# Prologue of a hybrid encoder layer: loads, statistics, normalisation, transposes and splits in another order

## The chip, the cores and the metric

The kernel runs on one core of one Trainium2 chip. The metric is the device time of one execution in microseconds (us). Three executions before the change took 1594.86, 1594.96 and 1596.01 us, with a median of 1594.96 us.

## The reference

The input x has 256 tokens of 4096 numbers in float32. It is normalised over its 4096 numbers per token (the embedding LayerNorm), goes through one layer, and is normalised again. Cut to what matters:

```python
h = layer_norm(x, emb_ln_g, emb_ln_b)
p = h @ w_in                       # (256, 4096) @ (4096, 13312)
# 16 channel groups of a gated short convolution, 16 attention heads (4 kv heads, window 128)
y_conv = c_b * centred_short_conv(c_c * c_h, conv_w) * silu(c_z)
y_attn = banded_window_attention(a_q, a_k, a_v, sink) * silu(a_z)
y = concatenate([y_conv, y_attn]) @ w_out     # (256, 4096) @ (4096, 4096)
out = layer_norm(2 ** 0.25 * h + y, ln_g, ln_b)
```

## The kernel before

The 256 tokens are two token tiles of 128 partitions, `xs[0]` and `xs[1]`, each of 128x4096. The transposed, normalised stream lies in `hT` as 32 blocks of 128 channels by 256 tokens. Matmuls contract over these blocks, and each result of 128 tokens by 512 columns is summed up in one PSUM accumulator over all 32 blocks.

The weights come in pieces of 1 MB (`load`, line 68): 128 partitions by 2048 numbers, that is, four blocks of 128 channels by 512 columns. Eight pieces make one chunk of 512 columns. A piece is split (`split`, line 77) into a high part `whi`, written by ScalarE (line 83), and a low part `wlo`, which VectorE makes by subtraction (line 85). The stream is split in the same way into `xT` (`x_split`, lines 206 and 207, both on VectorE). `mm` (line 105) then takes three matmuls for each block and token tile, in float32r (lines 116 to 118): 24 matmuls for one piece. For the raw pieces, the high parts and the low parts there are three buffers each.

The first two pieces are not split. They are loaded into two of the buffers of `whi` (the tiles `first`), and `first_mm` (line 198) multiplies them in plain float32 (line 201) with `hT`: `first_mm(q, i)` is piece q with token tile i, four matmuls, each of which the profile records twice. So pieces 0 and 1 need `hT` alone, and piece 2 is the first that needs `xT`, `whi` and `wlo`.

The order of the work is written out by hand: the program runs on each engine in the order of the code, and tiles carry the semaphores. The change touches the prologue, lines 135 to 262:

- `x_load(i)`, line 141: five loads of a token tile, all by SP's queue, in pieces of 1024, 1024, 1024, 512 and 512 columns. The weights come through the same queue. SP issues a load only when the eighth load before it has landed.
- `stats(i, c)`, line 161: VectorE's statistics of 512 columns, eight for a token tile. `stats_end(i)`, line 164: the aggregate, and `small_chain` (line 121), a chain of tiny instructions with one square root on ScalarE (line 124).
- `norm(i, q)`, line 168: 512 columns of a token tile are normalised in place, on VectorE or on GpSimd (line 170).
- `transp(i, q)`, line 173: TensorE turns four blocks of one token tile (line 177), and ScalarE takes each out of PSUM with the LayerNorm's gain and bias (line 180). `transp2(q)`, line 184: the same for both token tiles at once, with eight transposes (line 189) and four ScalarE instructions of twice the width (line 192).
- Two matmuls at line 214 run ahead of the transposes, for no result that is used.

In the order before, token tile 0 is normalised by VectorE (q = 0 to 2) and GpSimd (q = 3 to 7). VectorE takes the statistics of tile 1 in between, and their square root stands on ScalarE behind all sixteen instructions that take tile 0's first four groups out of PSUM. After the transposes of groups 0 to 3 of both tiles and the four `first_mm`, VectorE splits group 2 of the stream and piece 2 of the weights, and only then normalises the second half of tile 1 (the second `for q` over `norm(1, q)`). From piece 2 on, every step is `transp2` of a later group, `mm`, `x_split`, `split` and `load`.

Of the kernel before, what the change touches and what calls it, by code (L numbers as in the profile page):

```python
# [44 lines left out]
def encoder_kernel(ctx: ExitStack, tc: tile.TileContext, x, emb_g, emb_b, wi, conv_w, sink, wo, ln_g, ln_b, out):  # L45
    nc = tc.nc
# [5 lines left out]
    ps_acc = ctx.enter_context(tc.tile_pool(name="ps_acc", bufs=4, space=PSUM))  # L52
# [16 lines left out]
    def load(j, to=None):  # L69
        if j >= len(steps):  # L70
            return
        kind, a, b = steps[j]
        if to is None:
            to = raw[j] = wpool.tile([P, PIECE], F32, name="wraw")
        nc.sync.dma_start(out=to, in_=wi[a, b] if kind == "in" else wo[a + b])

    def split(j):
        if j >= len(steps):
            return
        w = raw.pop(j)  # L80
        over = j == len(steps) - 1
        wh[j] = wpool.tile([P, PIECE], F32R, name="whi", tag="wraw" if over else "whi")
        nc.scalar.activation(wh[j], w, AF.Copy)  # L83
        wl[j] = wpool.tile([P, PIECE], F32R, name="wlo", tag="wraw" if over else "wlo")
        nc.vector.tensor_tensor(wl[j], w, wh[j].bitcast(F32), op=ALU.subtract)  # L85


    ident = const.tile([P, P], F32, name="ident")
# [14 lines left out]
    acc = {}  # L103
# [31 lines left out]
    with tc.tile_pool(name="pro", bufs=1) as pro:  # L135
# [11 lines left out]
        nc.sync.dma_start(out=g_c, in_=emb_g)  # L147
        nc.sync.dma_start(out=b_c, in_=emb_b)
        load(0, first[0])
        x_load(1)  # L150
        load(1, first[1])
        for j in range(2, 4):
            load(j)
        nc.sync.dma_start(out=cw, in_=conv_w)
# [10 lines left out]
            nc.vector.bn_aggr(musd[:, i, 0:2], st[i])  # L165
            small_chain(musd[:, i:i + 1, :], 1)

        def norm(i, q, eng=None):
            sl = slice(q * 512, (q + 1) * 512)
            (eng or nc.vector).tensor_scalar(xs[i][:, sl], xs[i][:, sl], musd[:, i, 0:1], musd[:, i, 2:3],  # L170
                                             op0=ALU.subtract, op1=ALU.mult)

        def transp(i, q):
            pt = ps_att.tile([P, 4, P], F32, name="att")
            for k in range(4):
                kt = q * 4 + k
                nc.tensor.transpose(pt[:, k, :], xs[i][:, kt * P:(kt + 1) * P], ident)  # L177
            for k in range(4):
                kt = q * 4 + k
                nc.scalar.activation(hT[:, kt, i * P:(i + 1) * P], pt[:, k, :], AF.Identity, scale=g_c[:, kt:kt + 1],  # L180
                                     bias=b_c[:, kt:kt + 1])

        def transp2(q):
            for half in range(2):
                pt = ps_att.tile([P, 2, S], F32, name="att")
                for k in range(2):
                    kt = q * 4 + half * 2 + k
                    for i in range(2):
                        nc.tensor.transpose(pt[:, k, i * P:(i + 1) * P], xs[i][:, kt * P:(kt + 1) * P], ident)  # L189
                for k in range(2):  # L190
                    kt = q * 4 + half * 2 + k
                    nc.scalar.activation(hT[:, kt, :], pt[:, k, :], AF.Identity, scale=g_c[:, kt:kt + 1],
                                         bias=b_c[:, kt:kt + 1])
# [4 lines left out]
        def first_mm(q, i):  # L198
            for k in range(PK):
                kt = q * PK + k  # L200
                nc.tensor.matmul(acc[0, i], hT[:, kt, i * P:(i + 1) * P], first[q][:, k * W:(k + 1) * W],  # L201
                                 start=(kt == 0), stop=False)
# [9 lines left out]
        wu = ps_att.tile([P, 512], F32, name="att")  # L212
        for _ in range(2):
            nc.tensor.matmul(wu, ident, xs[0][:, 3072:3584], start=True, stop=True)
        for q in range(3, NQ):
            norm(0, q, nc.gpsimd)
        norm(0, 0)
        transp(0, 0)
        norm(0, 1)
        transp(0, 1)  # L220
        for c in range(NQ):
            stats(1, c)
            if c in (0, 2):
                if c == 0:
                    norm(0, 2)
                first_mm(c // 2, 0)
                transp(0, c // 2 + 2)
        stats_end(1)
        for q in range(NQ // 2):
            norm(1, q)  # L230
        transp(1, 0)
        transp(1, 1)
        first_mm(0, 1)
        transp(1, 2)
        transp(1, 3)
        first_mm(1, 1)
        x_split(2)
        split(2)
        load(5)
        for q in range(NQ // 2, NQ):  # L240
            norm(1, q)
        transp2(4)
        x_split(3)
        split(3)
        load(6)
        mm(2)
        transp2(5)
        x_split(4)
        split(4)
        load(7)  # L250
        mm(3)
        transp2(6)
        x_split(5)
        split(5)
        load(8)
        mm(4)
        transp2(7)
        x_split(6)
        split(6)
        load(9)  # L260
        mm(5)
        x_split(7)
        split(7)
        load(10)
# [407 lines left out]
```

## Time and profile before

| | |
|---|---|
| median of three executions | 1594.96 us |
| the profiled execution's own time | 1595.1 us |
| its span, from the first to the last instruction | 1593.4 us |
| matmuls on TensorE (PE) | 98% of the span |
| weight loads on TensorE (PEld) | 81% |
| VectorE (DVE) | 52% |
| ScalarE (ACT) | 39% |
| GpSimd (POOL) | 1% |
| read from HBM | 299.99 MB |

The profile comes from one execution. Its span lies 1.7 us under that execution's own time. "L118" is line 118 of the kernel. PE's rows are matmuls, PEld's are the loads of the stationary operand, SPq is the queue of SyncE, which issues the loads. A row of the timeline gives the start, the duration, the engine, the line, and what is written from what; at the end stands the idle time before it with what ended it. "PEclk" is the clock granted to TensorE as a share of full speed.

### The profile page before, as it was taken

The numbers are of one execution on the slowest core, as the hardware profiler recorded it, in microseconds if no ns is written. First come the engines' busy times: TensorE is split into PE (matmuls) and PEld (weight loads), VectorE is DVE, ScalarE is ACT, GpSimd is POOL, SyncE is SP. The second block draws the span as 40 slices with busy tenths as digits, with TensorE's granted clock in tenths as the row PEclk, the third lists the DMA queues.
The fourth block names the chain that finished last, engine by engine and source line by source line (L and its number), as shares of the span: only waits on it lengthen the run. The fifth ranks groups of instructions, "written<-read, shape, count | busy, mean of one in ns | idle before, by whom it ended". The sixth has DMA issues, their size and how long they took to land.

```text
span 1593.4 us, 16893 instructions
## 1 busy us (share of the span) xinstructions
PE 1567.2 (98%) x7182; PEld 1290.1 (81%) x7182; DVE 833.4 (52%) x702; ACT 620.3 (39%) x511; POOL 12.0 (1%) x12
## 2 busy tenths in 40 slices
PE   6999999999999999999999999999999999999997
PEld 3788888888888888888888888888888888888896
DVE  4754455464554645444544445444546556656656
ACT  3533435353444433333333333333344333333331
POOL 2000000000000000000000000000000000000000
PEclk9999999999999999999999999999999999999998
DMA  6555545545455455555555555555555657666662
GB/s 239 182 192 196 189 144 186 199 152 184 149 188 185 165 184 192 196 185 185 172 209 199 186 185 185 193 189 198 180 191 185 225 196 261 218 226 226 228 218 106
DMA packets 49515, 305.36 MB, mean 192 GB/s; under 512 B 6080, under 2 KB 7584, under 8 KB 14624
## 3 DMA queue, kind: packets, MB, share of 16 engines
q1 hardware_dynamic: 48864, 302.72, 54.6%
q10 hardware_dynamic: 576, 1.57, 0.3%
q8 instruction: 56, 0.92, 0.2%
q14 instruction: 19, 0.16, 0.0%
HBM read 299.99 MB, written 4.19 MB: 191 GB/s over the span
## 4 chain that ended last, share of the span: by engine, by line
PE 97%; DMA 1%; DVE 1%; ACT 0%; SPq 0%; issue 0%; DVEq 0%
PE acc L116 24%; PE acc L118 24%; PE acc L117 23%; PE acc L541 7%; PE acc L543 7%; PE acc L542 7%; PE att L305 1%; DMA first<-in_wi 1%; PE acc L201 1%; PE att L379 0%; DMA x<-in_x 0%; DVE R L576 0%; ACT hT L180 0%; PE att L189 0%; PE att L351 0%; PE att L390 0%
## 5 line engine op out<-in xcount | busy, mean ns | idle before, releaser
L85 DVE TENSOR_TENSOR wlo<-wraw,whi 128x2048 fp32r<-128x2048 f32 x270 | 618.0, 2291 | 628.7 <-ACT whi L83 628.6
L83 ACT ACTIVATE whi<-wraw 128x2048 fp32r<-128x2048 f32 x270 | 516.0, 1913 | 701.7 <-PE acc L118 439.9
L116 PE MATMUL acc<-whi,xT 128*128 128x512 f32 x1648 | 650.5, 395 | 0.0
L118 PE MATMUL acc<-whi,xT 128*128 128x512 f32 x1648 | 646.9, 393 | 0.0
L117 PE MATMUL acc<-wlo,xT 128*128 128x512 f32 x1648 | 641.8, 389 | 0.0
L118 PEld LDWEIGHTS acc<-whi,xT 128*128 128x128 f32 x1648 | 309.6, 188 | 70.6
L117 PEld LDWEIGHTS acc<-wlo,xT 128*128 128x128 f32 x1648 | 309.8, 188 | 68.1 <-DVE wlo L85 0.4
L116 PEld LDWEIGHTS acc<-whi,xT 128*128 128x128 f32 x1648 | 310.1, 188 | 61.9
L541 PE MATMUL acc<-whi,xT 128*128 128x512 f32 (+1 forms) x576 | 212.6, 369 | 0.0
L543 PE MATMUL acc<-whi,xT 128*128 128x512 f32 (+1 forms) x576 | 211.3, 367 | 0.0
L542 PE MATMUL acc<-wlo,xT 128*128 128x512 f32 (+1 forms) x576 | 209.8, 364 | 0.0
L543 PEld LDWEIGHTS acc<-whi,xT 128*128 128x128 f32 x576 | 108.0, 188 | 19.6
L542 PEld LDWEIGHTS acc<-wlo,xT 128*128 128x128 f32 x576 | 108.1, 188 | 19.1 <-DVE wlo L85 0.3
L541 PEld LDWEIGHTS acc<-whi,xT 128*128 128x128 f32 x576 | 108.3, 188 | 17.4 <-issue 0.7
L365 ACT ACTIVATE p<-s,nm 128x256 f32<-128x256 f32 x32 | 16.0, 502 | 59.8 <-DVE nm L360 59.8
L413 ACT ACTIVATE t<-att,cw 128x256 f32<-128x256 f32 x16 | 7.2, 474 | 26.8 <-PE att L305 16.1
L201 PE MATMUL acc<-first,hT 128*128 128x512 f32 x32 | 15.9, 640 | 1.2 <-DMA first<-in_wi 1.2
L180 ACT ACTIVATE hT<-att,b_c,g_c 128x128 f32<-128x128 f32 x32 | 11.7, 466 | 13.5 <-PE att L177 13.5
L391 DVE TENSOR_TENSOR Ya<-att,zT 128x256 f32<-128x256 f32 x16 | 6.7, 420 | 15.0 <-PE att L390 15.0
L414 DVE SCALAR_TENSOR_TENSOR t<-att,cw,t 128x255 f32<-128x255 f32 x16 | 7.7, 480 | 13.2 <-ACT t L413 13.2
L356 DVE SCALAR_TENSOR_TENSOR s<-tab,att 128x512 f32<-128x512 f32 x16 | 10.9, 681 | 5.8 <-PE att L353 5.8
L367 DVE TENSOR_TENSOR den<-den,es 128x2 f32<-128x2 f32 x16 | 2.6, 161 | 21.6 <-ACT es L366 21.6
(120 smaller groups left out, 473.7 us busy)
## 6 DMA issues: line engine op xcount, KB each, us to landing
wraw<-in_wi SPq DMA_DIRECT2D x206, 1024.0 KB, 4.9
wraw<-in_wo SPq DMA_DIRECT2D x64, 1024.0 KB, 5.0
xc<-in_x SPq DMA_DIRECT2D x14, 256.0 KB, 6.2
x<-in_x SPq DMA_DIRECT2D x6, 512.0 KB, 7.1
first<-in_wi SPq DMA_DIRECT2D x2, 1024.0 KB, 8.8
out<-R SPq DMA_DIRECT2D x4, 512.0 KB, 2.7
gb<-in_emb_g_row SPq DMA_DIRECT2D x7, 256.0 KB, 3.2
gb<-in_emb_b_row SPq DMA_DIRECT2D x7, 256.0 KB, 4.1
```

What stands on the lines that cost most here:

```text
L83: nc.scalar.activation(wh[j], w, AF.Copy)
L85: nc.vector.tensor_tensor(wl[j], w, wh[j].bitcast(F32), op=ALU.subtract)
L116: nc.tensor.matmul(a, xh, hk, start=(kt == 0), stop=False)
L117: nc.tensor.matmul(a, xh, lk, start=False, stop=False)
L118: nc.tensor.matmul(a, xl, hk, start=False, stop=(kt == KT - 1))
L180: nc.scalar.activation(hT[:, kt, i * P:(i + 1) * P], pt[:, k, :], AF.Identity, scale=g_c[:, kt:kt + 1], bias=b_c[:, kt:kt + 1])
L201: nc.tensor.matmul(acc[0, i], hT[:, kt, i * P:(i + 1) * P], first[q][:, k * W:(k + 1) * W], start=(kt == 0), stop=False)
L305: nc.tensor.transpose(ps[:, c, i * P:(i + 1) * P], t[:, i, (2 * b + c) * P:(2 * b + c + 1) * P], ident)
L365: nc.scalar.activation(p[:, b, :], s[:, b, :], AF.Exp, bias=nm[:, b:b + 1], accum_out=den[:, b:b + 1])
L541: nc.tensor.matmul(o, yh, hk, start=(s == 0), stop=False)
L542: nc.tensor.matmul(o, yh, lk, start=False, stop=False)
L543: nc.tensor.matmul(o, yl, hk, start=False, stop=(s == KT - 1))
```

## The change

Five things move; no arithmetic changes.

1. `split` becomes two functions, `split_hi` (ScalarE) and `split_lo` (VectorE), which can stand apart.
2. The load of the second `first` piece stands ahead of the five loads of token tile 1.
3. `norm` always runs on VectorE. All of tile 0 is normalised ahead of the statistics of tile 1, and all of tile 1 directly behind them.
4. `transp` only transposes, and `turned1` takes its PSUM tile out. For tile 1 those PSUM tiles come from the accumulators' pool. `transp2` can do one token tile at a time; `turned2` takes the pair out. Groups 2 and 3 are now turned by `transp2`, tile 0's half ahead of tile 1's statistics' end, tile 1's half later; before, `transp` did them.
5. From group 4 on, `transp2(q)` on TensorE keeps its place ahead of `mm(q - 2)`, but `turned2(q)` now stands behind that `mm` in the code, just ahead of `x_split(q)`. On ScalarE, `split_hi(2)` stands ahead of what takes tile 1 out of PSUM.

```diff
         load(0, first[0])
+        load(1, first[1])
         x_load(1)
-        load(1, first[1])
...
+        def turned1(i, q, pt):
             for k in range(4):
                 kt = q * 4 + k
                 nc.scalar.activation(hT[:, kt, i * P:(i + 1) * P], pt[:, k, :], AF.Identity, scale=g_c[:, kt:kt + 1],
                                      bias=b_c[:, kt:kt + 1])
...
+        def transp2(q, tiles=(0, 1)):
             for half in range(2):
-                pt = ps_att.tile([P, 2, S], F32, name="att")
+                if tiles[0] == 0:
+                    pair[q, half] = ps_att.tile([P, 2, S], F32, name="att")
...
-        for q in range(3, NQ):
-            norm(0, q, nc.gpsimd)
-        norm(0, 0)
-        transp(0, 0)
-        norm(0, 1)
-        transp(0, 1)
+        t0 = []
+        for q in range(2):
+            norm(0, q)
+            t0.append(transp(0, q, ps_att, "att"))
+        for q in range(2):
+            turned1(0, q, t0[q])
+            first_mm(q, 0)
+        for q in range(2, NQ):
+            norm(0, q)
         for c in range(NQ):
             stats(1, c)
-            if c in (0, 2):
-                if c == 0:
-                    norm(0, 2)
-                first_mm(c // 2, 0)
-                transp(0, c // 2 + 2)
+        transp2(2, (0,))
+        transp2(3, (0,))
         stats_end(1)
-        for q in range(NQ // 2):
+        split_hi(2)
+        for q in range(NQ):
             norm(1, q)
-        transp(1, 0)
-        transp(1, 1)
+        t1 = [transp(1, q, ps_acc, "acc") for q in range(2)]
+        transp2(2, (1,))
+        turned1(1, 0, t1[0])
         first_mm(0, 1)
-        transp(1, 2)
-        transp(1, 3)
+        transp2(3, (1,))
+        turned1(1, 1, t1[1])
         first_mm(1, 1)
+        turned2(2)
+        split_lo(2)
+        load(5)
         x_split(2)
-        split(2)
-        load(5)
-        for q in range(NQ // 2, NQ):
-            norm(1, q)
-        transp2(4)
+        turned2(3)
         x_split(3)
         split(3)
         load(6)
+        transp2(4)
         mm(2)
-        transp2(5)
+        turned2(4)
         x_split(4)
```

In the rows below, `x_88` and `x_89` are the token tiles 0 and 1, `first_91` and `first_92` the first two pieces of weights, `att` the PSUM tiles of transposes and `acc` the accumulators. The changed kernel's line numbers are shifted. TensorE before, from the first transposes to the transposes of group 4 (the row of L189 stands for the first of eight):

```order
L177 MATMUL att<-ident,x_88 128x128 x8
L201 MATMUL acc<-first_91,hT 128x512 x4
L177 MATMUL att<-ident,x_88 128x128 x4
L201 MATMUL acc<-first_92,hT 128x512 x4
L177 MATMUL att<-ident,x_88 128x128 x4
L177 MATMUL att<-ident,x_89 128x128 x8
L201 MATMUL acc<-first_91,hT 128x512 x4
L177 MATMUL att<-ident,x_89 128x128 x8
L201 MATMUL acc<-first_92,hT 128x512 x4
L189 MATMUL att<-ident,x_88 128x128
```

TensorE now, in the same place (L182 and L200 are the transposes, L217 is `first_mm`):

```order
L182 MATMUL att<-ident,x_88 128x128 x8
L217 MATMUL acc<-first_91,hT 128x512 x4
L217 MATMUL acc<-first_92,hT 128x512 x4
L200 MATMUL att<-ident,x_88 128x128 x8
L182 MATMUL acc<-ident,x_89 128x128 x8
L200 MATMUL att<-ident,x_89 128x128 x4
L217 MATMUL acc<-first_91,hT 128x512 x4
L200 MATMUL att<-ident,x_89 128x128 x4
L217 MATMUL acc<-first_92,hT 128x512 x4
L200 MATMUL att<-ident,x_88 128x128
```

Both pieces of tile 0 are multiplied in one go, and tile 0's groups 2 and 3 are turned behind them. ScalarE before, from the first square root to the first high part of weights:

```order
L124 ACTIVATE sd<-musd,eps_t 128x1
L180 ACTIVATE hT<-att,b_c,g_c 128x128 x16
L124 ACTIVATE sd<-musd,eps_t 128x1
L180 ACTIVATE hT<-att,b_c,g_c 128x128 x16
L83 ACTIVATE whi<-wraw 128x2048
L192 ACTIVATE hT<-att,b_c,g_c 128x256 x4
```

ScalarE now, in the same place (L129 is the square root, L80 the high part):

```order
L129 ACTIVATE sd<-musd,eps_t 128x1
L188 ACTIVATE hT<-att,b_c,g_c 128x128 x8
L129 ACTIVATE sd<-musd,eps_t 128x1
L80 ACTIVATE whi<-wraw 128x2048
L188 ACTIVATE hT<-acc,b_c,g_c 128x128 x8
L208 ACTIVATE hT<-att,b_c,g_c 128x256 x8
L80 ACTIVATE whi<-wraw 128x2048
```

The square root of tile 1 now has eight instructions ahead of it instead of sixteen, and the first high part stands ahead of tile 1's eight. VectorE before, from tile 0's normalisation to the second half of tile 1's, without the small chain:

```order
L170 TENSOR_SCALAR x_88<-x_88,musd 128x512 x2
L162 BN_STATS st_116<-x_89 128x6
L170 TENSOR_SCALAR x_88<-x_88,musd 128x512
L162 BN_STATS st_116<-x_89 128x6 x7
...
L170 TENSOR_SCALAR x_89<-x_89,musd 128x512 x4
L206 CAST xT<-hT 128x4x256
L207 TENSOR_TENSOR xT<-hT,xT 128x4x256
L85 TENSOR_TENSOR wlo<-wraw,whi 128x2048
L170 TENSOR_SCALAR x_89<-x_89,musd 128x512 x4
```

VectorE now, in the same place:

```order
L175 TENSOR_SCALAR x_88<-x_88,musd 128x512 x8
L167 BN_STATS st_116<-x_89 128x6 x8
...
L175 TENSOR_SCALAR x_89<-x_89,musd 128x512 x8
L85 TENSOR_TENSOR wlo<-wraw,whi 128x2048
L222 CAST xT<-hT 128x4x256
L223 TENSOR_TENSOR xT<-hT,xT 128x4x256
L222 CAST xT<-hT 128x4x256
L223 TENSOR_TENSOR xT<-hT,xT 128x4x256
L85 TENSOR_TENSOR wlo<-wraw,whi 128x2048
```

The eight normalisations of tile 1 stand together, ahead of the first low part and the first split of the stream.

More of the change, by code (lines that the diff above doesn't have):

```diff
@@ L75, in load, with split_hi, split_lo, split @@
         nc.sync.dma_start(out=to, in_=wi[a, b] if kind == "in" else wo[a + b])
[L77 to L80, printed above, removed]
+    def split_hi(j):
         over = j == len(steps) - 1
         wh[j] = wpool.tile([P, PIECE], F32R, name="whi", tag="wraw" if over else "whi")
-        nc.scalar.activation(wh[j], w, AF.Copy)
+        nc.scalar.activation(wh[j], raw[j], AF.Copy)
+    def split_lo(j):
+        over = j == len(steps) - 1
         wl[j] = wpool.tile([P, PIECE], F32R, name="wlo", tag="wraw" if over else "wlo")
-        nc.vector.tensor_tensor(wl[j], w, wh[j].bitcast(F32), op=ALU.subtract)
+        nc.vector.tensor_tensor(wl[j], raw.pop(j), wh[j].bitcast(F32), op=ALU.subtract)
+    def split(j):
+        if j < len(steps):
+            split_hi(j)
+            split_lo(j)
     ident = const.tile([P, P], F32, name="ident")
@@ L166, in stats_end, with norm, transp @@
             small_chain(musd[:, i:i + 1, :], 1)
-        def norm(i, q, eng=None):
+        def norm(i, q):
             sl = slice(q * 512, (q + 1) * 512)
[L170 to L174, printed above, removed]
+            nc.vector.tensor_scalar(xs[i][:, sl], xs[i][:, sl], musd[:, i, 0:1], musd[:, i, 2:3],
+                                    op0=ALU.subtract, op1=ALU.mult)
+        def transp(i, q, pool, name):
+            pt = pool.tile([P, 4, P], F32, name=name)
             for k in range(4):
@@ L177, in transp @@
                 nc.tensor.transpose(pt[:, k, :], xs[i][:, kt * P:(kt + 1) * P], ident)
+            return pt
+        def turned1(i, q, pt):
             for k in range(4):
@@ L181, in transp, with turned2 @@
                                      bias=b_c[:, kt:kt + 1])
-        def transp2(q):
+        pair = {}
+        def transp2(q, tiles=(0, 1)):
             for half in range(2):
-                pt = ps_att.tile([P, 2, S], F32, name="att")
+                if tiles[0] == 0:
+                    pair[q, half] = ps_att.tile([P, 2, S], F32, name="att")
                 for k in range(2):
                     kt = q * 4 + half * 2 + k
-                    for i in range(2):
-                        nc.tensor.transpose(pt[:, k, i * P:(i + 1) * P], xs[i][:, kt * P:(kt + 1) * P], ident)
+                    for i in tiles:
+                        nc.tensor.transpose(pair[q, half][:, k, i * P:(i + 1) * P], xs[i][:, kt * P:(kt + 1) * P],
+                                            ident)
+        def turned2(q):
+            for half in range(2):
+                pt = pair.pop((q, half))
                 for k in range(2):
@@ L250, in encoder_kernel @@
         load(7)
+        transp2(5)
         mm(3)
-        transp2(6)
+        turned2(5)
         x_split(5)
@@ L255, in encoder_kernel @@
         load(8)
+        transp2(6)
         mm(4)
-        transp2(7)
+        turned2(6)
         x_split(6)
@@ L260, in encoder_kernel @@
         load(9)
+        transp2(7)
         mm(5)
+        turned2(7)
         x_split(7)
```

## The prediction

> **What bounds the kernel now.** I read the page first, then the waits by engine, then the stretch in which TensorE waits: its timeline, the chain of work that ended last, and the timelines of VectorE and ScalarE.
>
> ```profile
> span 1593.4 us, 16893 instructions
> ...
> PE att L214 <- DMA x<-in_x: 8.9, 1, 8.9
> PE att L189 <- DVE x L170: 3.6, 1, 3.6
> PE att L177 <- DVE x L170: 3.2, 1, 3.2
> PE att L568 <- DVE t L563: 3.2, 1, 3.2
> PE acc L201 <- DMA first<-in_wi: 1.2, 1, 1.2
> ...
> 100.00:200.00 100.00, 100.00 (x443) 82.15 (x442) 42.88 (x21) 38.91 (x25) 0.00 (x0) 1.00 0.55 190
> ```
>
> The five middle rows are TensorE's waits over the whole run: microseconds in total, times, longest. The last row is a stage in the middle: 100 of 100 us busy at a granted clock of 1.00, VectorE and ScalarE under half. So outside the prologue and the tail nothing but TensorE's own work counts. The wait at L568 is in the tail, the 8.9 us at L214 are the first load; the change touches neither. It can win only the other three waits, 3.6 + 3.2 + 1.2 = 8.0 us, and what the clock loses behind them. TensorE's timeline there:
>
> ```profile
> 12.78 1.64 PE L177 MATMUL att<-ident,x 128*128 128x128 f32 x8
> 14.45 3.70 PE L201 MATMUL acc<-first,hT 128*128 128x512 f32 x8
> 17.98 0.60 PE L177 MATMUL att<-ident,x 128*128 128x128 f32 x4
> 19.80 3.67 PE L201 MATMUL acc<-first,hT 128*128 128x512 f32 x8 [1.22 <-DMA first<-in_wi]
> 27.12 1.57 PE L177 MATMUL att<-ident,x 128*128 128x128 f32 x8 [3.21 <-DVE x L170]
> 28.49 4.88 PE L201 MATMUL acc<-first,hT 128*128 128x512 f32 x8
> 33.20 1.04 PE L177 MATMUL att<-ident,x 128*128 128x128 f32 x8
> 34.08 3.60 PE L201 MATMUL acc<-first,hT 128*128 128x512 f32 x8
> 41.38 1.76 PE L189 MATMUL att<-ident,x 128*128 128x128 f32 x7 [3.60 <-DVE x L170]
> 42.79 0.78 PE L116 MATMUL acc<-whi,xT 128*128 128x512 f32 x1
> ...
> 49.24 1.03 PE L189 MATMUL att<-ident,x 128*128 128x128 f32 x8
> 50.03 0.48 PE L116 MATMUL acc<-whi,xT 128*128 128x512 f32 x1
> ...
> 55.63 1.03 PE L189 MATMUL att<-ident,x 128*128 128x128 f32 x8
> ...
> 28.00:29.00 1.00, 1.00 (x5) 0.79 (x4) 0.43 (x1) 1.00 (x4) 0.00 (x0) 0.50 0.00 0
> ...
> 42.00:43.00 1.00, 1.00 (x7) 1.00 (x6) 1.00 (x3) 0.68 (x2) 0.00 (x0) 0.50 0.62 139
> ```
>
> The two last rows are windows of 1 us; the 0.50 is the granted clock. After both longer waits the clock stands at half, and not after the wait of 1.22 us: `first_mm` takes 3.60 to 3.70 us in three of its four places (3.5 from start to the next start, 14.45 to 17.98), but 4.88 behind the wait of 3.21. The first `mm` (piece 2) takes 42.79 to 49.24 = 6.45 us, the second 50.03 to 55.63 = 5.60. Against full clock (0.88 for eight transposes, from 33.20 to 34.08), the cold stretches lose 28.49 - 27.12 - 0.88 = 0.5, 4.88 - 3.60 = 1.3, 42.79 - 41.38 - 0.79 = 0.6 (0.79 from 49.24 to 50.03) and 6.45 - 5.60 = 0.85: 3.25 us. With the waits, 11.25 us are there to be won.
>
> Why TensorE waits, by the chain of work that ended last:
>
> ```profile
> 9.80 9.86 DMA first<-in_wi
> ...
> 23.95 1.50 ACT hT L180 x4
> 25.45 0.19 ACT sd L124
> ...
> 36.75 1.81 ACT whi L83
> 38.58 2.29 DVE wlo L85
> 40.87 0.47 DVE x L170
> ```
>
> The second piece lands at 19.66. Only then come `first_mm(1, 0)`, the transposes of tile 0's group 3 and ScalarE's four instructions on them, and behind these ScalarE's square root for tile 1. VectorE had aggregated its statistics long before:
>
> ```profile
> 10.60 0.37 DVE L165 BATCH_NORM_AGGREGATE musd<-st 128x2 f32<-128x48 f32 x1
> ...
> 12.19 1.29 DVE L170 TENSOR_SCALAR x<-x,musd 128x512 f32<-128x512 f32 x2
> ...
> 14.71 4.23 DVE L162 BATCH_NORM_STATS2 st<-x 128x6 f32<-128x512 f32 x7
> ...
> 25.67 0.16 DVE L128 RECIPROCAL y<-sd 128x1 f32<-128x1 f32 x1 [6.13 <-ACT sd L124]
> ...
> 40.79 1.91 DVE L170 TENSOR_SCALAR x<-x,musd 128x512 f32<-128x512 f32 x4
> 42.62 0.68 DVE L206 CAST xT<-hT 128x1024 fp32r<-128x1024 f32 x1
> 43.33 1.23 DVE L207 TENSOR_TENSOR xT<-hT,xT 128x1024 fp32r<-128x1024 f32 x1
> ```
>
> VectorE stands 6.13 us for that square root. The second long wait is an order of VectorE: the second half of tile 1 is normalised only at 40.79, behind `whi` and `wlo` of piece 2.
>
> **The change, part by part.**
>
> *The load of the second piece ahead of tile 1.* Six megabytes land by 19.66 either way, since the queue is busy throughout:
>
> ```profile
> 10.00:20.00 10.00, 8.62 (x25) 4.09 (x24) 9.09 (x21) 4.58 (x13) 7.82 (x4) 1.00 1.02 416
> ...
> DMA to landing us min/median/max: 4.9/8.5/12.7
> ```
>
> At 416 GB/s a megabyte takes 2.5 us, a piece of 512 columns 0.6. I estimate the second piece at 14.6 (first piece 12.1), tile 1's pieces at 18.4 (third), 19.0 and 19.66 instead of all a megabyte earlier, by 17.2, and `wraw` of piece 2 at 22.2 as before. `first_mm(1, 0)` then follows the first at once, 17.98 to 21.5, and the wait of 1.22 us goes. Eight transposes of tile 0's groups 2 and 3 follow to 22.4. The loads' issue meets one more landing each, but nothing on SP stands behind them that is needed before 22.2.
>
> *Tile 0 on VectorE, statistics after it.* Four normalisations take 1.91 us (the row at 40.79), 0.46 each once they run one behind another; the first two beside GpSimd took 1.29. Eight take 3.7 us: 12.19 to 15.9. GpSimd's five go, and cost nothing, since TensorE needs groups 2 and 3 only at 21.5. Seven statistics took 4.23, 0.60 each: the first four run 15.9 to 18.3, the next two wait for the piece of 18.4, the last ends at 20.8. The aggregate follows; from the first tile's aggregate to its first normalisation it took 12.19 - 10.60 = 1.6 us, as ScalarE was free. It is free here too, as only eight of its instructions stand ahead, done by 17. So tile 1's normalisation begins at 22.4, not 26.5; transposes follow 0.6 later (12.19 to the first L177 at 12.78): 23.0 for group 0, 23.5 for group 1, 24.0 to 24.4 for tile 1's half of group 2.
>
> *`split_hi(2)` ahead of tile 1's exit from PSUM.* This is a wait added: ScalarE stands until `wraw` lands, and `turned1(1, 0)` is queued behind it, for which `first_mm(0, 1)` waits.
>
> ```profile
> 13.94 2.91 ACT L180 ACTIVATE hT<-att,b_c,g_c 128x128 f32<-128x128 f32 x8 [2.64 <-PE att L177]
> ...
> 36.60 1.95 ACT L83 ACTIVATE whi<-wraw 128x2048 fp32r<-128x2048 f32 x1
> ...
> 42.33 1.93 ACT L192 ACTIVATE hT<-att,b_c,g_c 128x256 f32<-128x256 f32 x4 [3.78 <-PE att L189]
> ```
>
> 22.2 + 1.95 + about 0.5 for the first of the eight gives 24.7 to 24.8 for `first_mm(0, 1)`. Without it the transposes would end last, at 24.4; so it costs 0.4. The bounds: 24.4, if the piece lands a little sooner, and 27.4, if the loads mix and it lands only with the next, 2.5 us later.
>
> *From there TensorE is the bound.* At full clock: `first_mm` 24.8 to 28.3, four transposes to 28.7, `first_mm(1, 1)` to 32.2, eight transposes of group 4 to 33.1, and `mm(2)` starts there instead of at 42.79. What it needs: ScalarE frees tile 1's groups at 27.1 (2.91 for eight from 24.2), group 2 at 29.1 (1.93) and group 3 at 31.0. VectorE ends its eight normalisations at 26.1, `split_lo(2)` (2.29) at 28.4, `x_split(2)` (0.68 + 1.23 on lines 206 and 207) at 31.0. So 2.1 us of cover; without it `mm(2)` would slip by what is missing. Next `split(3)`: `whi` at 33.0, `wlo` 35.3, for `mm(3)` at 39.5. Later steps need 3.9 us of ScalarE and 4.2 of VectorE per piece (1.93 + 1.95; 1.9 + 2.29), against 6.39 of TensorE (49.24 to 55.63). Load 5 is issued after `split_lo(2)`, at 28.4; even at the slowest landing, 12.7 us, it is there at 41.1, and its split stands on ScalarE behind the exit of group 5, which ends near 41.6 (39.6 + 1.93). Nothing falls due too late. The pair tiles and the accumulators that tile 1's transposes borrow are free by 27.1, long before the second chunk begins (33.1 and six pieces of about 6 us); I take them, and the later `turned2`, at nothing.
>
> *The sum.* Waits removed 8.0; the clock stays up, 3.25; new waits: 22.4 to 23.0 and 24.4 to 24.8, with rounding 0.9. That is 10.35, say 10.4 us. By starts: the transposes of group 5 come at 33.1 + 5.6 = 38.7 instead of 49.24, 10.5 us; the sums agree, and I keep the smaller. The profiled execution took 1595.1 (span 1593.4), 0.1 over the median of 1594.96; so 1595.1 - 10.4 = 1584.7 us.
>
> [...] The window of 10 to 20 us has a clock of 1.00 throughout, so from 17.98 to 19.80 it stayed up through 0.5 us of transposes and 1.22 of waiting. In the new order, 21.5 to 24.8 holds no plain matmul, only 16 + 4 transposes (about 2.2 us of them) and the two short waits. If transposes count as work, the clock has no reason to fall, and the sum stands. [...] The trace cannot settle it: no stretch of 3 us before holds mostly transposes.
>
> **The rivals.**
>
> 1. *The clock falls once more*, behind 21.5 to 24.8. For: the waits of 3.21 and 3.60 us did it. Against: the stretch is two thirds busy, and 1.22 us of waiting did nothing. It costs what the first cold stretch did to matmuls, 1.3 to 1.8 us: about 1586.4. Chance 0.13.
> 2. *Tile 1 or the third piece comes late.* The loads share 16 engines and may mix; tile 1's end or `wraw` lands up to 2.5 us later, and `first_mm(0, 1)` begins by 27.4: up to 1587.3. For: landing took 4.9 to 12.7 us. Against: the estimate already has every byte that is queued ahead of them landed first. Chance 0.10.
> 3. *The start is hidden anyway*: the weights, not TensorE, set the pace of pieces 3 to 9, and the 10.4 us come back as waits for `wlo`. Against: the budgets above, 4.2 against 6.39 us per piece, with 4 us in hand at piece 3. About 1595. Chance 0.03.
> 4. *Slower:* ScalarE stands at `split_hi(2)` with everything of tile 1 behind it, and the piece lands much later. From 22.2 on each microsecond costs one; to lose more than can be told, it must land after 22.2 + 10.4 + 3.2 = 35.8; at 15 us late it would be about 1599. For: it is the one wait that the change adds ahead of TensorE's work. Against: even if it landed last of all that is queued by then, behind pieces 3 and 4, that would be two megabytes later, at 27.2. Chance 0.02.
>
> **How the numbers follow.** The forecast has the remaining 0.72; its own range is 1583.6 (`first_mm(0, 1)` at 24.0 with the larger sum) to 1585.8. 0.2% is 3.2 us, about what can be told from no change. Faster by more than that: the forecast and rivals 1 and 2, 0.95; within it (rival 3) 0.03; slower (rival 4) 0.02. The range takes in rivals 1 and 2 nearly whole: 1583.4 to 1587.4.
>
> **What would show it right or wrong.** In the new profile: TensorE's waits for the normalisation (3.6, 3.2) and for the second piece (1.2) replaced by two under 1 us; the square root of tile 1 near 21; `first_mm(0, 1)` near 24.8; `mm(2)` near 33; the clock at 1.00 from 13 us on; no waits for `wlo` later. A clock of 0.50 behind 24.8 would be rival 1, `whi` of piece 2 starting well after 22.2 rival 2, waits at L122 or L123 rival 3. A gain under 7 us or over 12 would mean that the sum is wrong.

## The result and the profile after

| | kernel before | changed kernel |
|---|---|---|
| device time, median of the runs | 1595.07 us (1594.86 to 1596.01) | 1584.11 us (1583.93 to 1584.73) |
| time of the profiled execution | 1595.1 us | 1583.9 us |
| its span | 1593.4 us | 1582.2 us |
| transposes of group 5 start at | 49.24 us | 37.95 us |

The ratio is 0.9931, with a 95% interval of 0.9914 to 0.9948: faster by 11.0 us, where 10.4 was forecast (1584.7, in a range of 1583.4 to 1587.4). The last row is the one to compare traces by: from the transposes of group 5 on both kernels repeat the same steps with TensorE busy. It moved by 11.3 us, the spans by 11.2, so the whole gain is made in the prologue. Of these 11.3 us, 0.4 are luck: the first load landed sooner in this execution, and the first matmul started at 8.52 instead of 8.90. From the first matmul to group 5 it took 40.34 us and takes 29.43, 10.9 less.

From the page of the changed kernel, the span and three of TensorE's waits (total, times, longest):

```profile
span 1582.2 us, 16887 instructions
...
PE att L230 <- DMA x<-in_x: 8.5, 1, 8.5
PE att L590 <- DVE t L585: 3.2, 1, 3.2
PE acc L182 <- DVE x L175: 1.3, 1, 1.3
```

The first load and the wait in the tail (L590, before at L568) are left. Of the three waits between them, 3.6 + 3.2 + 1.2, one of 1.3 remains, for tile 1's normalisation. TensorE's timeline in the changed kernel (start, length, instruction, and in brackets the idle time ahead of it):

```profile
8.52 3.64 PE L230 MATMUL att<-x,ident 128*128 128x512 f32 x4 [8.52 <-DMA x<-in_x]
...
13.44 7.13 PE L217 MATMUL acc<-first,hT 128*128 128x512 f32 x16
20.41 1.04 PE L200 MATMUL att<-ident,x 128*128 128x128 f32 x8
22.72 1.11 PE L182 MATMUL acc<-ident,x 128*128 128x128 f32 x8 [1.28 <-DVE x L175]
23.67 0.62 PE L200 MATMUL att<-ident,x 128*128 128x128 f32 x4
24.16 3.70 PE L217 MATMUL acc<-first,hT 128*128 128x512 f32 x8
27.69 0.60 PE L200 MATMUL att<-ident,x 128*128 128x128 f32 x4
28.13 3.60 PE L217 MATMUL acc<-first,hT 128*128 128x512 f32 x8
31.57 1.04 PE L200 MATMUL att<-ident,x 128*128 128x128 f32 x8
32.36 0.48 PE L121 MATMUL acc<-whi,xT 128*128 128x512 f32 x1
...
37.95 1.03 PE L200 MATMUL att<-ident,x 128*128 128x128 f32 x8
```

From 22.72 on each line starts where the one before it ends (ends are modelled and overlap by some 0.2 us). Every `first_mm` takes 3.6 to 3.7 (the row at 13.44 is two of them), and the first `mm` 37.95 - 32.36 = 5.59 us with no cold stretch in it. A window of the changed kernel, with the granted clock as the third number from the right:

```profile
22.00:23.00 1.00, 0.28 (x3) 0.28 (x4) 0.96 (x4) 1.00 (x1) 0.00 (x0) 1.00 0.94 383
```

TensorE is only 28% busy between 22 and 23, and the clock stays at 1.00, as it does in every window of this prologue. Last ScalarE and, below it, VectorE in the changed kernel:

```profile
20.94 0.30 ACT L129 ACTIVATE sd<-musd,eps_t 128x1 f32<-128x1 f32 x1 [5.11 <-DVE musd L170]
21.84 1.92 ACT L80 ACTIVATE whi<-wraw 128x2048 fp32r<-128x2048 f32 x1 [0.61 <-DMA wraw<-in_wi]
```

```profile
15.46 5.04 DVE L167 BATCH_NORM_STATS2 st<-x 128x6 f32<-128x512 f32 x8
20.53 0.37 DVE L170 BATCH_NORM_AGGREGATE musd<-st 128x2 f32<-128x48 f32 x1
22.12 3.73 DVE L175 TENSOR_SCALAR x<-x,musd 128x512 f32<-128x512 f32 x8
25.77 2.28 DVE L85 TENSOR_TENSOR wlo<-wraw,whi 128x2048 fp32r<-128x2048 f32 x1
```

The roles have turned: before, VectorE stood 6.13 us for the square root of tile 1; now ScalarE stands 5.11 us for VectorE's statistics, and the root follows them at once (20.94, before 25.45). VectorE works without a wait from its statistics to 20.5 and sets the start of tile 1.

The gain closes with four numbers, from the prediction's rows and these. Tile 1's first transposes start at 22.72 instead of 27.12: 4.40. The second wait is gone: 3.60. From tile 1's transposes to group 5's it took 22.12 us, 18.52 without that wait, and takes 15.23: another 3.29, against 3.25 reckoned for the clock. Together 11.29 = 49.24 - 37.95. The 4.40 hold the 0.38 of the first load, and the 3.29 are not the clock alone, as the kernel with added matmuls shows below.

### The profile page after: what moved, and what is told of

Its sections match the earlier page's. It is cut to its first block, busy times and chain, and to the rows that moved or that the text cites. A ratio compares the mean times of both kernels' runs of the same rounds, so it can differ in the third digit from the quotient of the medians.

```text
span 1582.2 us, 16887 instructions
## 1 busy us (share of the span) xinstructions
PE 1563.1 (99%) x7182; PEld 1287.9 (81%) x7182; DVE 835.6 (53%) x707; ACT 618.1 (39%) x503; POOL 1.3 (0%) x7
## 4 chain that ended last, share of the span: by engine, by line
PE 98%; DMA 1%; DVE 1%; ACT 0%; issue 0%; DVEq 0%; SPq 0%
PE acc L121 24%; PE acc L123 24%; PE acc L122 24%; PE acc L563 8%; PE acc L565 7%; PE acc L564 7%; PE att L327 1%; DMA x<-in_x 1%; PE acc L217 0%; PE att L401 0%; DVE st L167 0%; DVE R L598 0%; PE att L200 0%; PE att L412 0%; PE att L373 0%; PE att L375 0%
## 5 line engine op out<-in xcount | busy, mean ns | idle before, releaser
L80 ACT ACTIVATE whi<-wraw 128x2048 fp32r<-128x2048 f32 x270 | 516.1, 1913 | 704.0 <-PE acc L123 441.5
L122 PE MATMUL acc<-wlo,xT 128*128 128x512 f32 x1648 | 640.8, 389 | 0.0
L122 PEld LDWEIGHTS acc<-wlo,xT 128*128 128x128 f32 x1648 | 309.5, 188 | 67.6
L208 ACT ACTIVATE hT<-att,b_c,g_c 128x256 f32<-128x256 f32 x24 | 11.5, 583 | 8.1 <-PE att L200 8.1
L217 PE MATMUL acc<-first,hT 128*128 128x512 f32 x32 | 14.4, 599 | 0.1
L378 DVE SCALAR_TENSOR_TENSOR s<-tab,att 128x512 f32<-128x512 f32 x16 | 10.9, 681 | 5.8 <-PE att L375 5.8
```

The costliest lines, as they stand in the source:

```text
L80: nc.scalar.activation(wh[j], raw[j], AF.Copy)
L122: nc.tensor.matmul(a, xh, lk, start=False, stop=False)
```

## The experiments

Two theories stood against each other. The prediction's: three waits, each with a cause of its own, and the clock behind two of them. The second: one chain (late square root, late exits and late `whi` on ScalarE, late `wlo` and normalisation on VectorE), in which a wait that is taken away alone is given back by the next link. Three kernels do one part alone in the kernel before, and a fourth keeps TensorE busy in its waits; six undo or load one part of the changed kernel. Ratios are to the kernel before, run on the same chip. Beside them, where the transposes of group 5 start in the profiled execution, and how long after the first matmul that is.

| kernel | time, us | ratio, 95% interval | group 5 at | from the first matmul |
|---|---|---|---|---|
| before | 1595.07 | | 49.24 | 40.34 |
| changed | 1584.11 | 0.9931 (0.9914 to 0.9948) | 37.95 | 29.43 |
| before + second piece loaded earlier | 1593.74 | 0.9990 (0.9981 to 0.9998) | 49.07 | 40.43 |
| before + square root earlier | 1591.95 | 0.9977 (0.9968 to 0.9987) | 45.80 | 37.08 |
| before + all of tile 1 normalised at once | 1593.05 | 0.9989 (0.9980 to 0.9998) | 45.82 | 37.20 |
| before + matmuls in the two waits | 1593.52 | 0.9989 (0.9980 to 0.9998) | 46.52 | 37.54 |
| changed, second piece loaded late | 1585.46 | 0.9938 (0.9925 to 0.9952) | 39.56 | 30.34 |
| changed, half of tile 1 normalised late | 1584.31 | 0.9928 (0.9915 to 0.9940) | 39.06 | 29.40 |
| changed, high part of piece 2 late | 1585.55 | 0.9937 (0.9924 to 0.9949) | 39.66 | 30.80 |
| changed + 48 transposes | 1587.77 | 0.9951 (0.9938 to 0.9963) | 42.26 | 33.41 |
| changed, tile 0 partly on GpSimd | 1584.52 | 0.9938 (0.9924 to 0.9952) | 38.70 | 29.92 |
| changed, second piece between tile 1's loads | 1584.18 | 0.9929 (0.9917 to 0.9942) | 38.38 | 30.07 |

None beat the changed kernel. In these kernels the first matmul starts between 8.3 and 9.7 us, as the first load lands; that is chance, it moves "group 5 at" by up to 1.1 us, and the last column is free of it. Each trace is one execution, though. And the changed kernel was not run again beside the last six: in their rounds the kernel before took 1595.8 and 1595.4 instead of 1595.07, and all their intervals overlap that of the changed kernel. So a difference of under a microsecond between their medians and 1584.11 says little.

### Before, with the second piece loaded earlier

```diff
         load(0, first[0])
+        load(1, first[1])
         x_load(1)
-        load(1, first[1])
```

> The kernel before with the second piece's load ahead of token tile 1, nothing else. Theory (the wait for the piece held up the square root of tile 1, which held up the next wait's end): the piece lands near 14.6, first_mm(1, 0) runs from 18.0 to 21.5, ScalarE leaves tile 0's group 3 at 23.6, the square root follows, and tile 1's first transposes start near 25.3 instead of 27.1: 1.8 us, so about 1593.3, with the clock still falling behind a wait of 3.3 us. Rival (only the wait of 1.2 us goes): 1593.9 and tile 1's transposes at 25.9. Rival (the load's place is worth the most of the 11 us): under 1590.

TensorE's timeline of this kernel, and two of its windows:

```profile
25.55 1.97 PE L177 MATMUL att<-ident,x 128*128 128x128 f32 x8 [3.21 <-DVE x L170]
27.32 5.76 PE L201 MATMUL acc<-first,hT 128*128 128x512 f32 x8
```

```profile
24.00:25.00 1.00, 0.00 (x0) 0.00 (x0) 0.76 (x6) 0.07 (x1) 0.00 (x0) 0.88 0.97 403
31.00:32.00 1.00, 1.00 (x2) 0.32 (x2) 0.00 (x0) 0.00 (x0) 0.00 (x0) 0.71 0.00 0
```

The wait for the piece is gone and tile 1's transposes start 1.6 us sooner (25.55, before 27.12). But the wait ahead of them stays at 3.21, and the cold stretch is longer: the clock falls late in the first of these windows and is back only late in the second, and `first_mm` takes 5.76 instead of 4.88. By group 5 only 0.17 us is left, and counted from the first matmul nothing. The 1.4 us by which this execution, whose time is the median, is faster come from elsewhere: the output projection's third line (L543) starts its first matmul at 1223.3 and its last at 1577.7, 354.4 us, before at 1223.5 and 1579.5, 356.0, which is told of at the end.

So it is luck that the median, 1593.74, lies between the expected 1593.3 and 1593.9. What this part alone is worth in the prologue stays open: the cold stretch was twice as long here as before (see the last section), which cost what the earlier transposes had won. An execution with a stretch as short as before would have kept about 1.3 us (an estimate, from 25.55 - 8.64 against 27.12 - 8.90).

### Before, with the square root earlier

```diff
-            if c in (0, 2):
-                if c == 0:
-                    norm(0, 2)
-                first_mm(c // 2, 0)
-                transp(0, c // 2 + 2)
+            if c == 0:
+                norm(0, 2)
+                first_mm(0, 0)
+                transp(0, 2)
         stats_end(1)
+        first_mm(1, 0)
+        transp(0, 3)
```

> The kernel before with first_mm(1, 0) and the transposes of tile 0's group 3 written behind the statistics' end of tile 1, so that the square root on ScalarE has twelve instructions ahead of it instead of sixteen; loads as before. Theory: the square root comes near 20, tile 1 is normalised from 21.2, its transposes start as soon as TensorE is free, at 23.9 instead of 27.1, and since there is no wait the clock stays up: 3.2 us and 1.8 us, about 1590.1, with the second wait (3.6 us) still there. Rival (the clock falls for another reason than the wait): 1591.9 and a granted clock of 0.50 near 25 to 28.

The square root starts at 19.42. TensorE's timeline:

```profile
20.11 3.67 PE L201 MATMUL acc<-first,hT 128*128 128x512 f32 x8 [2.11 <-DMA first<-in_wi]
23.62 1.47 PE L177 MATMUL att<-ident,x 128*128 128x128 f32 x12
26.16 3.70 PE L201 MATMUL acc<-first,hT 128*128 128x512 f32 x8 [1.07 <-ACT hT L180]
...
37.88 0.98 PE L189 MATMUL att<-ident,x 128*128 128x128 f32 x7 [3.60 <-DVE x L170]
```

Four transposes of tile 0 and eight of tile 1 now run without a break, so the first long wait is gone, as the prediction's reading of it wanted. Part of it comes back at once as a wait of 1.07 for ScalarE's exits. The second long wait is 3.60 to the digit as before, only 3.5 us sooner. Removing one link moved the rest of the chain and did not shorten it: 3.3 us from the first matmul to group 5, 3.2 in the median, where the theory had 5.0. The time happens to be the rival's, 1591.9, but not for the rival's reason: the clock is at 1.00 up to 39 us.

### Before, with all of tile 1 normalised at once

```diff
-        for q in range(NQ // 2):
+        for q in range(NQ):
             norm(1, q)
...
-        for q in range(NQ // 2, NQ):
-            norm(1, q)
         transp2(4)
```

> The kernel before with the second half of tile 1 normalised directly behind the first half, nothing else. As the prediction put it, the second wait is VectorE's order: then the whole 3.6 us and the cold start behind it go, about 5.0 us, 1590.1. Second theory: high and low part of piece 2 are late as well, since ScalarE takes them behind all of tile 1; the transposes of group 4 then start at 37.5, but the first mm waits for the low part until 40.9 instead of 42.8: 1.9 us, or 2.8 if the clock stays up through a wait of about 2.5 us, so 1592.3 to 1593.2, with TensorE waiting at the line of the low part.

TensorE's waits:

```profile
PE att L177 <- DVE x L170: 3.4, 2, 3.2
...
PE acc L117 <- DVE wlo L85: 1.8, 1, 1.8
```

The wait of 3.60 ahead of group 4 is gone and its cold stretch too (a granted clock of 1.00 in every window from 36 to 47 us), so the prediction had its direct cause. In its place stands a wait of 1.8 for `wlo` of piece 2, which ScalarE's late `whi` holds up. What is won up to group 5 is 3.1 us from the first matmul (2.1 in the median), not the 3.60 + 0.6 + 0.85 = 5.05 that the wait and its cold stretch cost. The second theory names what the prediction left out.

### Before, with matmuls in the two waits

```diff
+        wu = ps_acc.tile([P, W], F32, name="acc")
+        for _ in range(3):
+            nc.tensor.matmul(wu, ident, xs[0][:, 0:512], start=True, stop=True)
         transp(1, 0)
...
         for q in range(NQ // 2, NQ):
             norm(1, q)
+        wu = ps_acc.tile([P, W], F32, name="acc")
+        for _ in range(3):
+            nc.tensor.matmul(wu, ident, xs[0][:, 0:512], start=True, stop=True)
         transp2(4)
```

The result of the added matmuls is not used.

> The kernel before with three more matmuls of 128x512 (their result is used by nothing) ahead of tile 1's first transposes and three ahead of the transposes of group 4, so that TensorE works through 2.6 us of each long wait; no wait of the real work is shortened. Theory (3.25 us of the gain are the clock): granted clock 1.00 from 13 us on, and 0.5 + 1.3 + 0.6 + 0.85 us less, about 1591.8. Rival (the cold clock costs nothing of its own, as what is waited for sets the pace): no change, 1595.1.

TensorE's timeline, and one of its windows:

```profile
23.90 2.74 PE L233 MATMUL acc<-x,ident 128*128 128x512 f32 x6
27.27 1.11 PE L177 MATMUL att<-ident,x 128*128 128x128 f32 x8 [0.63 <-DVE x L170]
28.48 3.70 PE L201 MATMUL acc<-first,hT 128*128 128x512 f32 x8
...
40.19 0.98 PE L189 MATMUL att<-ident,x 128*128 128x128 f32 x7 [1.02 <-DVE x L170]
```

```profile
36.00:40.00 4.00, 3.17 (x9) 1.18 (x7) 2.76 (x3) 1.35 (x1) 0.00 (x0) 1.00 0.00 0
```

The useful work is as late as before (27.27 against 27.12), but the clock stays at 1.00 and `first_mm` takes 3.70 again. Group 5 comes 2.72 us sooner, 2.80 from the first matmul: this is the clock's share, measured apart from the waits, against 3.25 reckoned. Most of the difference is one term. At full clock too, `first_mm` starts 28.48 - 27.27 = 1.21 us behind tile 1's first transpose, not 0.88; before it was 28.49 - 27.12 = 1.37, so the cold clock cost 0.16 there and not 0.5. The median shows 1.6. In the profiled execution 0.9 us go to a wait for `wlo` in the output projection that the kernel before did not have; whether this is so in every run is open.

### Changed, with the second piece loaded late

```diff
         load(0, first[0])
-        load(1, first[1])
         x_load(1)
+        load(1, first[1])
```

> The changed kernel with the second piece's load back behind token tile 1. Theory: first_mm(1, 0) starts near 19.5 instead of 17.0 and ends at 23.0, tile 0's groups 2 and 3 are turned to 23.9, tile 1 is normalised from 21.9 and long ready, so its transposes follow without a wait and first_mm(0, 1) starts near 25.3 instead of 24.2: 1.1 us slower, about 1585.2, if a wait of 2.5 us does not drop the clock. Rival (the wait for the piece comes on top in full): 2.5 us, 1586.6. Rival (the clock falls): 1.3 us more.

TensorE's timeline:

```profile
20.18 3.67 PE L217 MATMUL acc<-first,hT 128*128 128x512 f32 x8 [2.13 <-DMA first<-in_wi]
23.69 1.04 PE L200 MATMUL att<-ident,x 128*128 128x128 f32 x8
24.56 1.04 PE L182 MATMUL acc<-ident,x 128*128 128x128 f32 x8
```

A wait of 2.13 for the piece takes the place of that for the normalisation, which is done by the time TensorE gets there. It costs 0.9 us from the first matmul to group 5, and 1.35 by medians: about a microsecond is what the earlier load is worth when the other parts are there, and behind 2.1 us of waiting the granted clock was 1.00, as in every window from 10 to 40 us.

### Changed, with half of tile 1 normalised late

```diff
-        for q in range(NQ):
+        for q in range(NQ // 2):
             norm(1, q)
...
         x_split(2)
+        for q in range(NQ // 2, NQ):
+            norm(1, q)
         turned2(3)
```

> The changed kernel with the second half of tile 1 normalised only behind the first split of the stream (x_split(2)), as before the change. By the prediction's reading the second wait comes from this order: TensorE waits for it again at the transposes of group 4, up to 3.6 us and a cold start, about 1588 to 1589. Second theory: with the high part of piece 2 taken early, VectorE is through its low part and x_split(2) at 30.3, normalises group 4 by 30.8, and the transposes of group 4 are due only at 31.6: no wait, 1584.1.

VectorE's row of the four late normalisations, and TensorE's rows of tile 1's first transposes, of `first_mm(0, 1)` and of the transposes that need the late normalisations:

```profile
31.38 1.91 DVE L175 TENSOR_SCALAR x<-x,musd 128x512 f32<-128x512 f32 x4
```

```profile
23.86 1.11 PE L182 MATMUL acc<-ident,x 128*128 128x128 f32 x8 [0.60 <-DVE x L175]
...
25.26 3.70 PE L217 MATMUL acc<-first,hT 128*128 128x512 f32 x8
...
32.67 1.04 PE L200 MATMUL att<-ident,x 128*128 128x128 f32 x8
```

VectorE has the second half of tile 1 behind piece 2 and the split of the stream, as before the change, and no wait comes of it: the first half of tile 1 is normalised and `whi` is made so much sooner that the second half, at 31.38, is just in time for 32.67. The time stays within the noise of the changed kernel's (1584.31 against 1584.11), and the way from the first matmul to group 5 is the same (29.40 against 29.43). So the prediction's "order of VectorE" was needed for the long wait, but not enough for it. It took a late ScalarE as well.

### Changed, with the high part of piece 2 late

```diff
         stats_end(1)
-        split_hi(2)
...
         turned2(2)
+        split_hi(2)
         split_lo(2)
```

> The changed kernel with the high part of piece 2 back behind what ScalarE takes out of PSUM for tile 1 and group 2. By the prediction it cost 0.4 us where it stood: 0.4 faster at first_mm(0, 1), 1583.7. Second theory: TensorE does not wait for it there, and moved back it makes the first mm late: ScalarE ends group 2 at 28.0, the high part at 29.9, VectorE the low part at 32.2 and x_split(2) at 34.1, where the first mm was due at 32.4: 1.7 us slower, about 1585.8, with TensorE waiting at the first mm.

TensorE's timeline, and below it a row of ScalarE's and a row of VectorE's:

```profile
24.45 3.60 PE L217 MATMUL acc<-first,hT 128*128 128x512 f32 x8
...
33.34 0.47 PE L121 MATMUL acc<-whi,xT 128*128 128x512 f32 x1 [0.53 <-DVE xT L222]
...
34.50 0.50 PE L123 MATMUL acc<-whi,xT 128*128 128x512 f32 x1 [0.46 <-DVE xT L223]
```

```profile
28.29 1.97 ACT L80 ACTIVATE whi<-wraw 128x2048 fp32r<-128x2048 f32 x1
```

```profile
30.29 2.29 DVE L85 TENSOR_TENSOR wlo<-wraw,whi 128x2048 fp32r<-128x2048 f32 x1 [4.11 <-ACT whi L80]
```

`first_mm(0, 1)` follows 1.40 us behind tile 1's transposes (24.45 against 23.05), in the changed kernel 1.44: there is no 0.4 to win. Late, `whi` at 28.29 leaves VectorE idle for 4.11 us, and `wlo` and the split of the stream come one behind the other: two waits of 0.5, and 1.4 us by group 5 and in the median. All five executions (1585.30 to 1586.01) lie above the four of the changed kernel. The one wait that the change adds for TensorE's path costs nothing where it stands and pays 1.4.

### Changed, with 48 more transposes

```diff
             pt = pool.tile([P, 4, P], F32, name=name)
+            if (i, q) == (1, 0):
+                for r in range(48):
+                    nc.tensor.transpose(pt[:, r % 4, :], xs[0][:, 0:P], ident)
```

The added transposes are overwritten by those that follow.

> The changed kernel with 48 more transposes (overwritten, used by nothing) ahead of tile 1's first, so that TensorE does nothing but transposes from 20.4 to about 28. If transposes count as work for the clock: 48 times 0.11 us, 5.3 us, of which 1.3 fill the wait for tile 1: 4.0 us slower, about 1588.1, and a granted clock of 1.00 throughout. If they do not count: the clock stands at 0.50 from about 24 on, the transposes take 0.2 us each and first_mm(0, 1) 4.7 us or more: 1590 or later.

TensorE's timeline, and two windows of 2 and 3 us:

```profile
21.14 1.04 PE L203 MATMUL att<-ident,x 128*128 128x128 f32 x8
22.01 5.40 PE L182 MATMUL acc<-ident,x 128*128 128x128 f32 x48
...
28.56 3.60 PE L220 MATMUL acc<-first,hT 128*128 128x512 f32 x8
```

```profile
22.00:24.00 2.00, 2.00 (x21) 2.00 (x20) 1.90 (x8) 1.70 (x1) 0.00 (x0) 1.00 1.03 408
24.00:27.00 3.00, 3.00 (x30) 3.00 (x29) 3.00 (x7) 0.23 (x1) 0.00 (x0) 1.00 0.81 324
```

From 21.14 to 28.56, 7.4 us, TensorE does nothing but transposes, 68 of them; the clock stays at 1.00, and the `first_mm` behind them runs at its full 3.60. By medians it costs 3.7 us, by group 5 4.0: 5.2 us of transposes less the wait of 1.3 that they fill.

Whether transposes count as work for the clock was left open by the prediction. Here the granted clock is 1.00 in every window from 20 to 30 us, with 7.4 us of fp32 transposes in them; in the kernel before it was at 0.50 behind a wait of 3.21 us. For these transposes that is the expectation's first case, and it speaks against rival 1.

### Changed, with tile 0 partly on GpSimd, and with the second piece between tile 1's loads

The first gives groups 3 to 7 of tile 0 back to GpSimd; the second takes the load of the piece to between the second and the third load of tile 1. The helpers' new arguments are left out here.

```diff
-        for q in range(2, NQ):
-            norm(0, q)
+        norm(0, 2)
+        for q in range(3, NQ):
+            norm(0, q, nc.gpsimd)
```

> The changed kernel with tile 0's parts 3 to 7 normalised on GpSimd again. Theory (taking them off GpSimd neither cost nor won): VectorE is free at 13 instead of 15.4, but tile 1's first piece lands at 15.4 and the statistics start where they did; TensorE needs part 3 only at 20: no change, 1584.1, within 0.3. Rival (GpSimd slows VectorE, as in the profile before, where two normalisations beside it took 1.29 us instead of 0.92): tile 1's transposes come later by as much as the statistics are slowed, 0.5 to 1.5 us, 1584.6 to 1585.6.

```diff
-        load(1, first[1])
-        x_load(1)
+        x_load(1, 0, 2)
+        load(1, first[1])
+        x_load(1, 2)
```

> The changed kernel with the second piece's load between the second and the third piece of tile 1. The piece lands near 16.7, just ahead of first_mm(1, 0) at 17.0; tile 1's first two pieces land 2.5 us earlier, the other three where they did. Theory (the statistics' end is set by VectorE's eight in a row from the first piece's landing): they start at 15.4, behind tile 0's normalisation, in any case, and end where the last pieces let them: 0 to 0.5 us faster, 1583.6 to 1584.1. Rival (the piece lands late for TensorE): up to 1 us slower.

VectorE's statistics of tile 1, in the first kernel and then in the second:

```profile
16.23 5.04 DVE L167 BATCH_NORM_STATS2 st<-x 128x6 f32<-128x512 f32 x8 [2.38 <-DMA x<-in_x]
```

```profile
15.32 2.46 DVE L168 BATCH_NORM_STATS2 st<-x 128x6 f32<-128x512 f32 x4
18.38 2.47 DVE L168 BATCH_NORM_STATS2 st<-x 128x6 f32<-128x512 f32 x4 [0.60 <-DMA x<-in_x]
```

In the first kernel VectorE has less to do and spends the difference waiting 2.38 us for tile 1's first load; the eight statistics then take the same 5.04, so GpSimd does not slow them, against the rival, though the median, 0.4 above the changed kernel's, lies between theory and rival. In the other, half of tile 1 lands sooner and the rest as late as ever, a wait of 0.60 stands in the middle, and the statistics end at 20.85 instead of 20.50. TensorE's wait stays at 1.1 and 1.3, and both times stay within the noise. So who normalises tile 0 does not set the remaining wait. In the changed kernel the statistics follow tile 0's normalisation without a break; take that work away and the landing of tile 1's first load sets their start, bring half of the load forward and the other half sets their end.

## Why the prediction was right, and where it was off

- *What bounds it.* Right: all of the gain lies ahead of group 5.
- *The load of the second piece.* The wait of 1.22 is gone, as said. Put back in the changed kernel it costs about a microsecond (0.9 up to group 5, 1.35 by medians). Alone in the kernel before it won 1.4 in the median, and nothing in the prologue of the one execution that was traced.
- *Tile 0 on VectorE, statistics after it.* Eight normalisations took 3.74 (3.7 reckoned), and the chain to tile 1 came as worked out, 0.06 to 0.3 us sooner at each step: root 20.94 (near 21), normalisation 22.12 (22.4), transposes 22.72 (23.0). The statistics were to wait for the last pieces and end at 20.8; they ran without a break and ended at 20.50. That they were 0.3 sooner is luck: tile 0's aggregate, from which the chain starts, came at 10.04 instead of 10.60, as the first load landed sooner. GpSimd's work was rightly costed at nothing.
- *`split_hi(2)`.* The step was mis-sized: 0.4 was charged, and nothing was paid. `whi` began at 21.84 instead of 22.2, and `first_mm(0, 1)` came at 24.16 right behind the transposes, not at 24.8. The sooner first load does not explain it: in the kernel with half of tile 1 normalised late the first matmul came as late as 9.66, and `first_mm(0, 1)` followed tile 1's first transposes by the same 1.40 us (25.26 against 23.86). `whi` started 0.9 us ahead of those transposes in both, close to the 0.8 reckoned; what was put too long is the way from `whi`'s start to `first_mm(0, 1)`: 2.6 reckoned, 2.3 in both. Where the instruction stands it is worth 1.4 us, by the kernel that has it late. The prediction had the cover behind it right in kind (2.1 us in hand for VectorE), but did not say that the early `whi` is what gives it.
- *New waits.* Two of together 0.9 were forecast; it is one of 1.28, which begins sooner because TensorE is done with tile 0 at 21.4 instead of 22.4. One reason can be seen: the first matmul started 0.38 sooner, and from it to the first `first_mm` took 13.44 - 8.52 = 4.92 us instead of 14.45 - 8.90 = 5.55. It shows in the wait and not in the time, since the wait ends with the normalisation, at 22.72 against 23.0.
- *The clock.* Right in direction, and some 0.4 too large: 3.25 forecast, 2.8 by the added matmuls. The 3.29 that is left in the changed kernel's rows hold about 0.4 from the new order of the transposes besides. Rival 1 fell: 3.75 us without a plain matmul (20.41 to 24.16) left the clock at 1.00, and so did 7.4.
- *The second long wait as an order of VectorE.* The part of the reading that failed as a full cause. Changing that order alone put a wait of 1.8 for `wlo` in its place, and keeping the old order in the changed kernel cost nothing. What made the wait was the lateness of ScalarE and VectorE together. The early square root alone left it at 3.60, so the early `whi` is the likely cure; that is argued, as no kernel has it alone. The sum did not suffer, as the change does all of it.
- *Rivals 2 to 4.* No late landing (`whi` at 21.84), no wait for `wlo` at L122, no loss from ScalarE standing at `split_hi(2)`, for 0.61 us.

By starts, the prediction was 0.75 us late at group 5 (38.7 against 37.95). About half is the first load, 0.38, which is luck; counted from the first matmul 29.8 was forecast and 29.43 came, about the price of `split_hi(2)` that was not paid. The other sum, by waits and clock, came out near for a worse reason: the clock was put 0.4 too high and the new waits 0.4 too low, and some 1.3 us were not reckoned at all, the 0.6 up to the first `first_mm` and the 0.4 from the order of the transposes among them.

## What to carry to other kernels

Waits in a chain that runs through several engines are not worth their length one by one: the three parts that were tried alone won 1.4, 3.2 and 2.1 us in the median, 6.8 together, and the whole change 11.0. Which parts need each other for the rest was not tried, as no kernel has two of them. Look for the short instruction (here a square root of 0.3 us) that an engine's order holds behind work for somebody else: VectorE stood 6.13 us for it. And count the cold stretch behind a wait as part of the wait (here 3.41 us or more at a clock of 0.50 behind each of the six waits of 3.2 and 3.6 us), but do not add its price to that of a wait that is only moved.

## What the runs showed of the hardware

- In these prologues, the granted clock was 1.00 behind waits of 1.2 to 2.1 us on TensorE, and fell to 0.50 with each of the six of 3.2 and 3.6 us. The first wait, for the first load, shows no fall: 8.9 us in the kernel before and 8.5 in the changed one, at 1.00 in all windows from 0 to 9 us.
- How long it stayed at 0.50 differs. Two windows of the kernel before:

```profile
27.00:28.00 1.00, 0.88 (x6) 0.84 (x7) 1.00 (x4) 0.14 (x1) 0.00 (x0) 0.80 0.04 16
31.00:32.00 1.00, 1.00 (x4) 0.46 (x3) 0.00 (x0) 0.00 (x0) 0.00 (x0) 0.99 0.00 0
```

A mean of 0.80 means 0.4 us at half clock, so the clock fell at 27.60; it was back at 31.01 (by finer windows): 3.41 us. In the kernel with the second piece loaded earlier the windows of 0.88 and 0.71 give 24.76 and 31.58: 6.82 us, twice as long, behind a wait of the same 3.21. The four others, by windows of 1 and 2 us, are 41.25 to 44.66 in the kernel before, 41.82 to 45.24 in that with the piece loaded earlier, 39.08 to 42.48 in that with the square root earlier and 26.44 to 29.86 in that with all of tile 1 normalised at once: 3.41 each, to 0.01. The six begin 2.4 to 4.8 us after their wait does. So the same wait of 3.21 us had twice the cold stretch in one execution, with a `first_mm` of 5.76 instead of 4.88 behind it; what sets its length and its start is not shown. Nor is it shown why 31 executions of the kernel before, run beside its four variants, spread over 3.9 us and four of the changed kernel over 0.8.

- 48 fp32 transposes of 128x128 ran in 5.40 us, 0.11 each, with 20 others around them, and the granted clock was 1.00 in every window from 20 to 30 us.
- From the first to the last start of its third line, the output projection took 354.4 and 354.5 us in two of the profiled executions (the kernels with the piece loaded earlier and with half of tile 1 normalised late), and 355.9 to 357.0 in the others. In the second of the two its 256-column matmuls started 0.113 us apart from 1525 to 1555 us, in the changed kernel 0.118; for the first of the two the starts are not shown. The difference is worth about 1.5 us, as much as the earlier load won alone, and is not explained. It is one reason for reading the experiments by the start of group 5 beside the medians.
